# A hybrid decoder trunk on one core: 16x16 blocks of a triangular inverse moved packed, and a short convolution done by tokens from shifted copies in DRAM

## The chip, the cores and the metric

One core of one Trainium2 chip runs the whole program. The metric is the device time of one execution in microseconds; the figure for a kernel is the median of several executions. The profile shows one more execution, with the time of every instruction on the engines: TensorE (PE, its weight loads PEld), VectorE (DVE), ScalarE (ACT), GpSimd (POOL), SyncE (SP). SP does nothing but issue transfers; ACT issues some as well, between its own instructions.

## The reference

Two layers over 256 tokens of width 2048. What matters here is the gated DeltaNet branch:

```
hn   = rms_norm(h, norm_w[l]);  proj = hn @ w_in[l]                 # 8208 columns
qkv  = silu(causal_conv(proj[:, :3072], conv_w))                     # width 4, per channel, over tokens
q, k = l2_norm(q) * 128**-0.5, l2_norm(k);  v = heads(v)             # 8 heads of 128
A    = strict_lower((k * beta) @ k.T * decay)                        # per head, chunks of tokens
u, w = triangular_solve(A + I, [v * beta, k * beta * exp(G)])
...  state recurrence over chunks, o = q_decay @ state + qk @ v_new
y    = concat(gated_head_norm(o, z), hgrn2_branch(...))              # 8 heads each
h    = h + y @ w_out[l]
h    = h + (p[l] @ w_ple_up[l]) * sigmoid(h @ w_ple_gate[l])
```

The other branch (HGRN2) reads the same projection, and a last RMSNorm ends the trunk. All is float32.

## The kernel before

**The matrix products.** Each weight tile is loaded as float32 into a buffer `raw` (three buffers), and split into a high part `whi` (ACT, line 405) and a rest `wlo` (DVE, line 407), three buffers each. A product is three TensorE passes: activation high with weight high, high with rest, rest with high (line 341). The weights are cut into 392 steps in a fixed order (`make_plan`): per layer 128 steps of the input projection, 32 of the output projection, 36 of gate and embedding. A step of 512 columns holds two row tiles of 128 and makes twelve passes of 128x512. `run_step` calls `ahead`, which issues loads up to four steps ahead on SP's queue (line 383) as far as the three buffers allow, and splits two steps ahead, and then makes the step's products.

**The side work.** Everything else is written as generators (`DN`, `HG`, `Inverse`). A generator does a piece of work and yields a number of steps to wait, from the table `DELAY` (overridden per head group by `DELAY_AT`); `tick` at the end of each step counts these down. So their TensorE instructions stand at fixed places between the steps, in the order in which the program issues them. On the other engines a planner orders the instructions at build time by its own estimate of when each is ready, the earlier one of the program first; at run time each engine takes its list in order.

**Values of DeltaNet** (`DN.dv`, four head groups `g` a layer, two heads each). `evict` (line 602) scales the projected values by the row's RMS factor into `vet`; `turned` makes four TensorE transposes into PSUM (`pvc`, line 344), so that tokens lie along the free axis; `conv` then makes the width-4 convolution with two ACT instructions (line 790) and six DVE instructions (line 794), and a sigmoid; line 880 multiplies the two; four more transposes (`pv`) turn the result back, and line 887 scales it by `invn` into `R`. With `R` and the inverse `Tt` the recurrence goes on (`pz`, `pS`, `pw`, `pz`, `po`, then `yt`, `yp` and the split of `y`).

**Inverse** (one per layer, 16 blocks of 128x128 in `Bt`). The 16x16 blocks on the diagonal are inverted by substitution on DVE with one block per partition (`fx`); to get there they go through DRAM: each group's `Bt` is written to `d1` and read back by diagonal blocks. The result goes back the same way: line 659 stores `X` into the diagonal blocks of a DRAM area `d2` that was cleared at the start (line 298, four transfers of 256 KB), and line 661 loads all of `d2`, zeros included, as `Tt` (1 MB), both from ACT's queue and without a yield between. After `T` steps the blocks are merged to 32, 64 and 128 with transposes on DVE (lines 670, 694, 719, 720) and small TensorE products (`pp`, `px`).

**Buffers.** The split activations of every product live in one pool `acts` with 13 buffers of each part: 8 for the normed input, then those of `y`, of the residual, of the embedding. PSUM has three banks for products and five for side work.

## Time and profile before

| | |
|---|---|
| time, median of 3 runs | 1256.82 us (1256.73 to 1257.85) |
| profiled execution, its own time | 1258.06 us |
| its span, first to last instruction | 1256.3 us |
| mean granted clock of TensorE | 0.995 |
| TensorE busy | 1234.1 us (98%), 8385 matmuls |
| VectorE busy | 881.4 us (70%) |
| ScalarE busy | 780.3 us (62%) |
| moved by DMA | 221.59 MB, 176 GB/s over the span |

Busy time is the time in which an engine worked on an instruction; matmuls overlap, so a row of 0.39 us can be followed by the next one 0.23 us later, and the distance of two starts is what a matmul costs. All times in the rows are microseconds from the start of the span unless marked ns.

### The profile page before, as it was taken

The page shows a single profiled execution, that of the slowest core. Times are in us where ns is not written, and L with a number is a line of the kernel's source. Part 1 is how long each engine was busy: PE and PEld are TensorE (multiplying, and loading weights), DVE is VectorE, ACT ScalarE, POOL GpSimd, SP SyncE. Part 2 cuts the span into 40 slices and gives each one's busy share as a digit, 9 for nine tenths or more (in the row PEclk, how much of TensorE's full clock was granted, in tenths as well). Part 3 has the DMA queues.
Part 4 walks back from the last instruction along what each step waited for, and adds up shares of the span by engine and source line. Part 5 has one row for each costly group of instructions (what it writes and reads, how often), then busy time and mean ns, then how long its engine had stood idle before and what let it go on. Part 6 is the DMA issues. An engine that isn't in the chain of part 4 may idle for free.

```text
span 1256.3 us, 21606 instructions
## 1 busy us (share of the span) xinstructions
PE 1234.1 (98%) x8385; PEld 1035.4 (82%) x8385; DVE 881.4 (70%) x1520; ACT 780.3 (62%) x1399; POOL 68.6 (5%) x57
## 2 busy tenths in 40 slices
PE   9999999899999999999999999999999999999996
PEld 7878887698888888888888888887988888888886
DVE  7777796868667755546667877968776596565566
ACT  7567675576666754447556767666776676444465
POOL 0310000000000000000003100000000000000010
PEclk9999999999999999999999999999999999999999
DMA  8565556345455555555565556555455546655563
GB/s 283 191 217 196 177 166 210 121 135 163 141 167 168 167 169 180 190 190 185 185 185 170 176 176 176 171 186 170 124 163 152 170 149 202 195 183 184 184 201 134
DMA packets 76375, 221.59 MB, mean 176 GB/s; under 512 B 15344, under 2 KB 22384, under 8 KB 76272
## 3 DMA queue, kind: packets, MB, share of 16 engines
q1 hardware_dynamic: 59040, 211.52, 53.4%
q10 hardware_dynamic: 17232, 8.69, 2.5%
q8 instruction: 66, 1.08, 0.4%
q14 instruction: 37, 0.30, 0.1%
HBM read 214.67 MB, written 5.51 MB: 175 GB/s over the span
## 4 chain that ended last, share of the span: by engine, by line
PE 85%; DVE 6%; ACT 4%; DMA 3%; issue 2%; ACTq 0%; SPq 0%; DVEq 0%
PE out L341 14%; PE gate L341 13%; PE in1hf L341 7%; PE in1dk L341 7%; PE in0dv L341 6%; PE in1dv L341 6%; PE in0hf L341 5%; PE in1hi L341 5%; PE in0hi L341 4%; PE in0dk L341 4%; DMA raw<-W 3%; DVE wlo L407 2%; PE up L341 2%; ACT whi L405 1%; PE in1dz L341 1%
## 5 line engine op out<-in xcount | busy, mean ns | idle before, releaser
L407 DVE TENSOR_TENSOR wlo<-raw,whi 128x1024 fp32r<-128x1024 f32 (+1 forms) x392 | 482.0, 1232 | 289.2 <-ACT whi L405 287.8
L405 ACT ACTIVATE whi<-raw 128x1024 fp32r<-128x1024 f32 (+1 forms) x392 | 411.7, 1052 | 342.0 <-PE out L341 89.5
L341 PE MATMUL in1hi<-whi,n1hi 128*128 128x512 f32 x128 | 51.5, 403 | 0.0
L341 PE MATMUL in1hf<-whi,n1hi 128*128 128x512 f32 x128 | 51.4, 402 | 0.0
L341 PE MATMUL in1dk<-whi,n1hi 128*128 128x512 f32 x128 | 51.1, 399 | 0.0
L341 PE MATMUL in1hf<-wlo,n1hi 128*128 128x512 f32 x128 | 50.0, 391 | 1.0 <-DVE wlo L407 1.0
L341 PE MATMUL in1hi<-wlo,n1hi 128*128 128x512 f32 x128 | 50.2, 392 | 0.0
L341 PE MATMUL gate<-whi,g0hi 128*128 128x512 f32 x128 | 50.1, 392 | 0.0
L341 PE MATMUL in1hi<-whi,n1lo 128*128 128x512 f32 x128 | 50.0, 390 | 0.0
L341 PE MATMUL in1dk<-whi,n1lo 128*128 128x512 f32 x128 | 50.0, 390 | 0.0
L341 PE MATMUL in1hf<-whi,n1lo 128*128 128x512 f32 x128 | 49.9, 390 | 0.0
L341 PE MATMUL in1dk<-wlo,n1hi 128*128 128x512 f32 x128 | 49.9, 390 | 0.0
L341 PE MATMUL gate<-whi,g0lo 128*128 128x512 f32 x128 | 49.8, 389 | 0.0
L341 PE MATMUL gate<-wlo,g0hi 128*128 128x512 f32 x128 | 49.8, 389 | 0.0
L341 PE MATMUL in1dv<-whi,n1hi 128*128 128x512 f32 (+1 forms) x128 | 48.0, 375 | 0.0
L341 PE MATMUL in1dv<-whi,n1lo 128*128 128x512 f32 (+1 forms) x128 | 46.6, 364 | 0.0
L341 PE MATMUL in1dv<-wlo,n1hi 128*128 128x512 f32 (+1 forms) x128 | 46.5, 363 | 0.0
L341 PE MATMUL gate<-whi,g1hi 128*128 128x512 f32 (+1 forms) x120 | 45.5, 379 | 0.0
L341 PE MATMUL gate<-wlo,g1hi 128*128 128x512 f32 (+1 forms) x120 | 45.4, 379 | 0.0
L341 PE MATMUL gate<-whi,g1lo 128*128 128x512 f32 (+1 forms) x120 | 45.4, 378 | 0.0
L341 PE MATMUL in0hi<-wlo,n0hi 128*128 128x512 f32 x96 | 38.4, 400 | 2.4 <-DVE wlo L407 2.3
L341 PE MATMUL in0hi<-whi,n0hi 128*128 128x512 f32 x96 | 39.2, 409 | 0.0
(1496 smaller groups left out, 3177.9 us busy)
## 6 DMA issues: line engine op xcount, KB each, us to landing
raw<-W SPq DMA_DIRECT2D x384, 512.0 KB, 3.5
raw<-W SPq DMA_DIRECT2D x7, 544.0 KB, 3.7
h<-x SPq DMA_DIRECT2D x4, 512.0 KB, 4.8
xt<-xT SPq DMA_DIRECT2D x3, 512.0 KB, 6.3
out_dram<-h SPq DMA_DIRECT2D x6, 256.0 KB, 2.4
d<-zero ACTq DMA_DIRECT2D x4, 256.0 KB, 7.3
di0d<-di0Bt ACTq DMA_DIRECT2D x4, 256.0 KB, 2.8
di1d<-di1Bt ACTq DMA_DIRECT2D x4, 256.0 KB, 2.3
```

The costliest lines, as they stand in the source:

```text
L341: return tc.keep_in_program_order(nc.tensor.matmul(*a, **k))
L405: S.activation(hi[:, sl], raw[:, sl], AF.Copy)
L407: V.tensor_tensor(lo[:, sl], raw[:, sl], hi[:, sl].bitcast(F32), ALU.subtract)
```

## The change

Four things are changed.

1. The blocks of `Inverse` are moved packed: `X` is stored to `d2` as 128 KB without gaps; after `w` = 2 steps eight transfers on ACT's queue load the diagonal 16x16 blocks from there into `Tt`, 16 partitions each (256 pieces of 64 bytes). The zeros of `Tt` come from four GpSimd memsets at the start of `Inverse.run`. The clearing of the old `d2` is gone. The merge begins 6 steps after the loads (8 after the store), where it began 11 and 13 after.
2. `DN.dv` convolves by tokens, without transposes: `vet` is stored to DRAM (256 KB, ACT's queue) behind three rows of zeros; 2 steps later SP's queue loads the convolution's weights, spread over all partitions (`cvw`, 512 KB, one buffer), and three copies shifted by one, two and three tokens (256 KB each). 3 steps on (5 for group 0 of both layers) DVE makes four multiplications and three additions of 128x512, then the sigmoid, and 2 steps on four instructions of 128x128 that multiply by the sigmoid and `invn` into `R`. `R` is written 8 steps after the group's columns are done (10 for group 0), where it was 6 (7).
3. The loads of the residual input (`xtok`, four of 512 KB on SP's queue) move from steps 22 to 31 to steps 92 to 112 of the loads.
4. `acts` has 12 buffers where it had 13 (the room goes to `cvw`), and some delays change (`h0x4`, `h0o`, `h1c`, `h3q`, `d0z1`, `d1y`, `d1yp`, `d2D`, `i0p32`).

```diff
--- before.py
+++ after.py
@@ -36,23 +36,24 @@
 
 
 DELAY = {
-    "d": {'c': 1, 'D': 4, 'k': 6, 'q': 7, 'ssq': 1, 'v': 5, 'z0': 1, 'S': 1, 'w': 1, 'z1': 1, 'o': 1, 'y': 3, 'yp': 1},
-    "i": {'F': 4, 'F2': 1, 'F3': 1, 'F4': 1, 'T': 12, 't16': 3, 'p16': 2, 't32': 3, 'p32': 2, 't64': 3, 'p64': 2},
+    "d": {'c': 1, 'D': 4, 'k': 6, 'q': 7, 'ssq': 1, 'vl': 2, 'vc': 3, 'v2': 1, 'v': 2, 'z0': 1, 'S': 1, 'w': 1, 'z1': 1, 'o': 1, 'y': 3, 'yp': 1},
+    "i": {'F': 4, 'F2': 1, 'F3': 1, 'F4': 1, 'w': 2, 'T': 6, 't16': 3, 'p16': 2, 't32': 3, 'p32': 2, 't64': 3, 'p64': 2},
     "b": {'o': 1, 'g': 4},
     "h": {'c': 1, 'f': 1, 'x2': 1, 'x4': 1, 'x8': 1, 'a': 2, 'x16': 1, 'x32': 1, 'x64': 1, 'u16': 2, 'u64': 1, 'o': 2, 'y': 2, 'yp': 1, 'q': 0},
 }
 
 DELAY_AT = {
     "b1g": 5,
-    "d0D": 3, "d0c": 2, "d0q": 6, "d0y": 2,
-    "d2D": 3, "d2k": 4, "d2o": 2, "d2q": 9, "d2y": 2,
+    "d0D": 3, "d0c": 2, "d0q": 6, "d0vc": 5, "d0y": 2, "d0z1": 3,
+    "d1y": 4, "d1yp": 3,
+    "d2k": 4, "d2o": 2, "d2q": 9, "d2y": 2,
     "d3D": 5, "d3ssq": 2,
-    "h0c": 2, "h0o": 4, "h0u64": 3, "h0y": 3,
-    "h1c": 3, "h1o": 1, "h1q": 1, "h1x32": 2, "h1yp": 3,
+    "h0c": 2, "h0o": 3, "h0u64": 3, "h0x4": 3, "h0y": 3,
+    "h1c": 4, "h1o": 1, "h1q": 1, "h1x32": 2, "h1yp": 3,
     "h2c": 2, "h2q": 2,
-    "h3u64": 2, "h3x2": 2,
-    "i0T": 11, "i0p16": 1, "i0t16": 5,
-    "i1T": 13, "i1t16": 2,
+    "h3q": 1, "h3u64": 2, "h3x2": 2,
+    "i0p16": 1, "i0p32": 1, "i0t16": 5,
+    "i1t16": 2,
 }
 
 
@@ -164,12 +165,12 @@
-    ap_ = pool("acts", 13)
+    ap_ = pool("acts", 12)
@@ -218,10 +219,10 @@
         7: lambda: x_(3),
         9: lambda: first(cs, cst),
         17: lambda: first(ms, msk),
-        22: lambda: xtok(0),
-        25: lambda: xtok(1),
-        28: lambda: xtok(2),
-        31: lambda: xtok(3),
+        92: lambda: xtok(0),
+        96: lambda: xtok(1),
+        108: lambda: xtok(2),
+        112: lambda: xtok(3),
     }
 
     def first_loads():
@@ -279,7 +280,9 @@
 
     dr = pool("scratch", 1, space=bass.MemoryType.DRAM)
 
-    d2 = dr.tile([16512 * 4 * NG], F32, name="d2")
+    d2 = dr.tile([256 * 128], F32, name="d2")
+
+    dsh = [dr.tile([256 * 259], F32, name=f"dsh{j}") for j in range(2)]
     dfull = lambda d: d.rearrange("(i x) -> i x", i=4 * NG)[:, 0:16384].rearrange("i (p c) -> p i c", c=128)
     ddiag = lambda d: d.rearrange("(q x) -> q x", q=32 * NG)[:, 0:2048].rearrange("q (s f) -> q s f", s=16)[:, :, 0:16]
     SLr = cp.tile([128, 128], F32R, name="SLr")
@@ -287,16 +290,15 @@
     hA = cp.tile([128, 4, 128], F32, name="hA")
 
     def clear_scratch():
+        zero = sp.tile([128, 6], F32, tag="zero", name="zero", bufs=1)
+        G.memset(zero, 0.0)
+        for d in dsh:
+            tc.keep_in_program_order(nc.scalar.dma_start(out=d[0:768].rearrange("(p f) -> p f", p=128), in_=zero))
 
         V.tensor_scalar(SLr, UI, -1.0, 1.0, ALU.mult, ALU.add)
         G.memset(hA[64:128, :, 0:64], 0.0)
         for b in (0, 64):
             G.memset(hA[b + 32:b + 64, :, b:b + 32], 0.0)
-        zero = tp.tile([128, 512], F32, tag="tmp", name="zero")
-        G.memset(zero, 0.0)
-        for j in range(NG):
-            tc.keep_in_program_order(nc.scalar.dma_start(out=dfull(d2)[:, 4 * j:4 * j + 4],
-                                                         in_=zero.rearrange("p (i c) -> p i c", i=4)))
 
     def P(name, i, n=1):
         o = PAR[name][0] + i
@@ -643,6 +645,9 @@
             n, Bt, NT = self.n, self.Bt, self.NT
 
 
+            Tt = self.Tt = v4(mix("Tt", 128 * NT, 1, n + "Tt"))
+            for j in range(0, NT, 4):
+                G.memset(Tt[:, j:j + 4], 0.0)
             fx = tmp(n + "fx").rearrange("q (w a b) -> q w a b", w=2, a=16)
             F, X = fx[:, 0], fx[:, 1]
             nc.scalar.dma_start(out=X, in_=eye)
@@ -656,9 +661,12 @@
                 if c == 1:
                     tc.keep_in_program_order(i)
                 V.tensor_reduce(X[:, :c, c:c + 1], pr_[:, :c, :c], mybir.AxisListType.X, ALU.add)
-            nc.scalar.dma_start(out=ddiag(d2), in_=X)
-            Tt = self.Tt = v4(mix("Tt", 128 * NT, 1, n + "Tt"))
-            nc.scalar.dma_start(out=Tt, in_=dfull(d2))
+
+            nc.scalar.dma_start(out=d2.rearrange("(q a c) -> q a c", q=128, a=16), in_=X)
+            yield self.wait("w")
+            for j in range(8):
+                b = slice(16 * j, 16 * j + 16)
+                nc.scalar.dma_start(out=Tt[b, :, b], in_=d2.rearrange("(i b a c) -> b a i c", i=NT, b=8, a=16)[j])
             yield self.wait("T")
 
 
@@ -874,17 +882,40 @@
 
         def dv(self, ps, c0):
             n, kq, g = self.n, self.kq, self.g
-            et = evict(ps, c0, 256, self.row.rt, n + "v")
-            yield self.wait("c")
-            ac, sg = self.conv(turned(et, 0, n + "pvc"), 2)
-            V.tensor_tensor(ac, ac, sg, ALU.mult)
+
+
+            full = mix("et", 1024, 2, n + "vet")
+            et, x1 = full[:, :512], full[:, 512:]
+            d = dsh[g % 2]
+            for t in range(2):
+                sl = slice(256 * t, 256 * t + 256)
+                S.activation(et[:, sl], ps[t][:, c0:c0 + 256], AF.Copy, scale=self.row.rt[:, t:t + 1])
+            v2 = lambda ap: ap.rearrange("p (t n) -> p t n", t=2)
+            rows = lambda j: d[256 * (3 - j):256 * (259 - j)].rearrange("(t p n) -> p t n", t=2, p=128)
+            nc.scalar.dma_start(out=rows(0), in_=v2(et))
+            wv = mix("cvw", 1024, 1, n + "cvw")
+            yield self.wait("vl")
+            nc.sync.dma_start(out=wv, in_=cvw[self.l * NG + g])
+            xs = [x1, tmp(n + "vs2"), tmp(n + "vs3")]
+            for j, x in enumerate(xs, 1):
+                nc.sync.dma_start(out=v2(x), in_=rows(j))
+            yield self.wait("vc")
+            w = lambda j: bc1(wv[:, 256 * j:256 * j + 256], 2)
+            V.tensor_tensor(v2(et), v2(et), w(3), ALU.mult)
+            for j, x in enumerate(xs, 1):
+                V.tensor_tensor(v2(x), v2(x), w(3 - j), ALU.mult)
+                V.tensor_tensor(et, et, x, ALU.add)
+                if j == 1:
+                    yield self.wait("v2")
+            sigmoid(x1, et)
             yield self.wait("v")
             yield self.after("k")
-            pv = pm.tile([128, 512], F32, tag="m", name=n + "pv")
+
+            R = v4(mix("R", 512, 2, n + "R"))
             for i in range(4):
-                PE.transpose(pv[:, 128 * i:128 * i + 128], ac[:, 128 * i:128 * i + 128], ident)
-            R = v4(mix("R", 512, 2, n + "R"))
-            V.tensor_tensor(R, v4(pv), bc(self.invn, 128), ALU.mult)
+                hh, t = divmod(i, 2)
+                sl = slice(256 * t + 128 * hh, 256 * t + 128 * hh + 128)
+                V.scalar_tensor_tensor(R[:, i], et[:, sl], self.invn[:, i:i + 1], x1[:, sl], ALU.mult, ALU.mult)
             yield lambda: self.inv.ready
             yield self.wait("z0")
             Tt = self.inv.Tt[:, 4 * g:4 * g + 4]
@@ -1389,6 +1420,9 @@
+        "cvw": np.ascontiguousarray(np.broadcast_to(
+            a["dn_conv_w"][:, :, 2048:].reshape(DEPTH, 4, NG, 256).transpose(0, 2, 1, 3).reshape(DEPTH * NG, 1, 1024),
+            (DEPTH * NG, 128, 1024))),
```

## Rows read from the trace of the kernel before

**Rows 1.** The page: busy time of the engines, with their share of the span and their instructions; and the chain that ended last, by engine.

```profile
PE 1234.1 (98%) x8385; PEld 1035.4 (82%) x8385; DVE 881.4 (70%) x1520; ACT 780.3 (62%) x1399; POOL 68.6 (5%) x57
...
PE 85%; DVE 6%; ACT 4%; DMA 3%; issue 2%; ACTq 0%; SPq 0%; DVEq 0%
```

**Rows 2.** The waits of TensorE in the whole span, longest first: who it waited for, us in total, times, the longest.

```profile
PE in0hi L341 <- DVE wlo L407: 2.3, 1, 2.3
PE dn00pg L341 <- DVE dn00kq L802: 1.9, 1, 1.9
PE in0hf L341 <- issue: 1.8, 1, 1.8
PE hg00yp L344 <- DVE hg00yt L580: 1.4, 1, 1.4
...
PE in1hf L341 <- DVE wlo L407: 1.0, 1, 1.0
...
PE di0px L341 <- issue: 0.7, 1, 0.7
```

**Rows 3.** TensorE in order of time around one group of four transposes of the values: start, us, engine, line, operation.

```profile
902.54 0.60 PE L344 MATMUL dn10pvc<-cs,dn10vet 128*128 128x128 f32 x4
902.90 0.48 PE L341 MATMUL in1dv<-whi,n1hi 128*128 128x512 f32 x1
903.21 0.39 PE L341 MATMUL in1dv<-wlo,n1hi 128*128 128x512 f32 x1
903.45 0.40 PE L341 MATMUL in1dv<-whi,n1lo 128*128 128x512 f32 x1
```

**Rows 4.** Three stretches: from:to, length, busy us (x instructions) of PE, PEld, DVE, ACT, POOL, granted clock, DMA share, GB/s. The first two follow the blocks' store and load in layer 0, the last is an even stretch with values of DeltaNet in it.

```profile
200.00:212.00 12.00, 12.00 (x63) 10.32 (x64) 5.62 (x5) 5.97 (x9) 0.00 (x0) 1.00 0.66 229
...
222.00:232.00 10.00, 7.66 (x27) 5.83 (x26) 9.26 (x18) 4.64 (x10) 0.00 (x0) 0.83 0.32 107
...
960.00:990.00 30.00, 30.00 (x144) 25.03 (x143) 17.91 (x27) 19.28 (x35) 1.30 (x1) 1.00 0.55 164
```

**Rows 5.** ACT in order of time in layer 0 from the store of `X` (line 659) to the weight splits that follow; in square brackets the idle time before an instruction and what ended it.

```profile
192.76 0.37 ACTq L659 DMA_DIRECT2D d<-di0fx  x1
...
196.56 0.02 ACT L661 MOVE_SHAPE di0Tt<-d  x1 [1.88 <-DMA d<-di0fx]
196.62 0.81 ACTq L661 DMA_DIRECT2D di0Tt<-d  x1
197.56 1.06 ACT L405 ACTIVATE whi<-raw 128x1024 fp32r<-128x1024 f32 x1 [0.97 <-PE hg00pa L341]
...
207.62 1.06 ACT L405 ACTIVATE whi<-raw 128x1024 fp32r<-128x1024 f32 x1 [5.68 <-DMA raw<-W]
```

**Rows 6.** The same place on TensorE (a step begins at 199.53), and TensorE after its longest wait, which ended at 226.30.

```profile
199.53 0.39 PE L341 MATMUL in0hi<-whi,n0ahi 128*128 128x512 f32 x1
199.93 0.50 PE L341 MATMUL in0hi<-wlo,n0ahi 128*128 128x512 f32 x1
...
227.26 0.63 PE L341 MATMUL in0hi<-wlo,n0hi 128*128 128x512 f32 x1
227.69 0.63 PE L341 MATMUL in0hi<-whi,n0lo 128*128 128x512 f32 x1
```

**Rows 7.** Transfers: target and source, queue, how many, KB each, median us from issue to landing.

```profile
raw<-W SPq DMA_DIRECT2D x384, 512.0 KB, 3.5
...
d<-zero ACTq DMA_DIRECT2D x4, 256.0 KB, 7.3
...
d<-di0fx ACTq DMA_DIRECT2D x1, 128.0 KB, 3.8
...
di0Tt<-d ACTq DMA_DIRECT2D x1, 0.5 KB, 8.1
```

**Rows 8.** The issuing alone of the four transfers that clear `d2`, one behind the other on ACT's queue: ns min/median/max, first and last start.

```profile
L298 ACTq DMA_DIRECT2D d<-zero x4: 393/593/786, 28.2 to 30.2; - x4
```

**Rows 9.** Single DVE operations, ns min/median/max, start, forms: the convolution, a product of 128x512 from SBUF, an instruction of 128x128 with a factor per partition.

```profile
L794 DVE SCALAR_TENSOR_TENSOR dn01vac<-dn01pvc,pr,dn01vac x6: 458/478/482, 312.7 to 315.2; 128x255 f32<-128x255 f32 x2, 128x254 f32<-128x254 f32 x2, 128x253 f32<-128x253 f32 x2
...
L880 DVE TENSOR_TENSOR dn02vac<-dn02vac,dn02vsg x1: 685/685/685, 375.8 to 375.8; 128x512 f32<-128x512 f32 x1
...
L580 DVE SCALAR_TENSOR_TENSOR dn00yt<-dn00o,fo,dn00sz x4: 343/344/352, 327.8 to 328.6; 128x128 f32<-128x128 f32 x4
```

**Rows 10.** One weight step beside the values of group 2 in layer 0, each line from the order of time of its engine: the end of the eviction of these values; the step's load (the second of the two in the row), its split on ACT and on DVE, its second product on TensorE, the first that needs the rest.

```profile
361.75 0.47 ACT L602 ACTIVATE dn02vet<-in0dv,s0rt 128x256 f32<-128x256 f32 x1 [0.52 <-PE in0dv L341]
...
364.82 2.33 SPq L383 DMA_DIRECT2D raw<-W  x2
...
373.63 1.04 ACT L405 ACTIVATE whi<-raw 128x1024 fp32r<-128x1024 f32 x1
...
374.70 1.23 DVE L407 TENSOR_TENSOR wlo<-raw,whi 128x1024 fp32r<-128x1024 f32 x1 [1.65 <-ACT whi L405]
...
379.04 0.40 PE L341 MATMUL in0hf<-wlo,n0hi 128*128 128x512 f32 x1
```

**Rows 11.** TensorE in order of time where its third chunk begins.

```profile
42.93 0.50 PE L341 MATMUL in0dk<-whi,n0ahi 128*128 128x512 f32 x1 [0.73 <-ACT dn00kqet L602]
```

**Rows 12.** The sixth split activation of `y` in layer 0: its transposes on TensorE, and the ACT instruction that reads them.

```profile
L344 PE MATMUL dn02yp<-cs,dn02yt x4: 272/273/273, 407.5 to 407.8; 128*128 128x128 f32 x4
...
L496 ACT ACTIVATE dn02hi<-dn02yp,pr x1: 690/690/690, 415.2 to 415.2; 128x512 fp32r<-128x512 f32 x1
```

More of the change, by code (lines that the diff above doesn't have):

```diff
@@ L166, in trunk @@
 @with_exitstack
-def trunk(ctx: ExitStack, tc: tile.TileContext, head, xT, x, pT, W, par, fw, cst, msk, eye, out):
+def trunk(ctx: ExitStack, tc: tile.TileContext, head, xT, x, pT, W, par, cvw, fw, cst, msk, eye, out):
     nc = tc.nc
```

## The prediction

> **What bounds the kernel now.** I read the page first. TensorE is busy for 98% of the span and makes 85% of the chain that ended last [rows 1]. So only two things can shorten the run: fewer TensorE instructions, or shorter waits of TensorE. Work taken off another engine gains nothing unless TensorE waits for it.
>
> I then read TensorE's waits. They are few, and most stand in one place: the waits for `hg00yt`, for `wlo` under in0hi, for "issue" under in0hf and under di0px [rows 2] all fall between 213 and 243 us, while layer 0's Inverse is in progress. Layer 1 has a single one over 0.3 us there, 1.0 us (in1hf). The remaining one of size, 1.9 us for `dn00kq`, is at the start.
>
> Third, I followed that cluster back on ACT [rows 5]. The store of `X` is issued at 192.76. ACT's next DMA, the load of `Tt`, must wait for it to land: ACT stands idle for 1.88 us and then issues for 0.81 us, so that a weight split starts at 197.56 that could have started at 194.7. Behind it the 1 MB load takes 8.1 us to land [rows 7], and the weight loads share the DMA engines with it: the split at 207.62 comes after 5.68 us of idling for `raw<-W`. DVE and ACT are then a step behind, and TensorE pays up to 30 us later. The DMA share of 0.66 at 229 GB/s [rows 4] puts full DMA at some 229 / 0.66 = 347 GB/s.
>
> **The change: transposes.** Each group of values loses two bursts of four transposes. A burst starts at 902.54 and the next product at 902.90, 0.36 us; that product is followed after 0.31 us by one that would come after 0.23, another 0.08 [rows 3]. With 8 groups and 2 bursts, 16 x 0.44 = 7.1 us leave TensorE. Nothing hides them: it has no idle time beside them.
>
> **The Inverse.** The four waits in layer 0 add up to 2.3 + 1.8 + 1.4 + 0.7 = 6.2 us [rows 2]. A row of idle time counts from the modelled end of a product, 0.39 us after its start, where the next would have started 0.23 us after it [rows 3], so each wait costs 0.16 more: 0.6. After the longest wait products stand 0.43 us apart [rows 6] and the stretch 222 to 232 has a mean granted clock of 0.83 [rows 4]: at half clock (1.2 GHz) that is 0.34 of 10 us, which loses 1.7. Layer 0 pays 8.5 us, layer 1 1.0 + 0.16 = 1.2. The store and the pieces are 128 KB now, the pieces are an eighth of the 1 MB, and two steps (2 x 12 passes x 0.23 = 5.5 us) stand between store and load, where a store of 64-byte pieces landed in 3.8 [rows 7]. The merge moves 3 and 5 steps earlier, so its bursts of small products no longer stand next to those of `hg01pa` or `hg11pa` in the same places; the two waits for "issue" have no other releaser in the profile, and I let them go with the rest, between nothing and all of their 2.8 us. Gain 9.7.
>
> What comes instead is eight issues on ACT's queue in a row, with weight splits queued behind them. One alone takes 0.37 us [rows 5]; the four that clear `d2` grow from 0.39 to 0.79 as they follow each other [rows 8]. So ACT is held for 8 x 0.37 = 3.0 to 8 x 0.79 = 6.3 us, plus between 0 and 1.9 for the store, against 1.88 + 0.81 = 2.7 now. The present hold leaves TensorE just short: at 199.53 the step's first product comes in time, the second, which needs the rest, 0.40 later where 0.23 is normal [rows 6]. So every microsecond more is paid at once, if the planner puts the loads where the old load stood: between 0.3 and 5.5 a layer. Nothing is lost if the two steps move them to a better place, since a split can begin two steps, 5.5 us, before it is needed. I take 2 us a layer, nearer the lower end, because the delay of two steps lies above the landing of 3.8: 4.0 in all.
>
> **Values through DRAM.** On DVE seven instructions of 128x512 at 0.69 and four of 128x128 at 0.34 make 6.2 us; six at 0.48 go, one of 0.69, and line 887, which I price like it: 4.3 [rows 9]. DVE gets 1.9 us more per group and is busy 17.91 of 30 us in a stretch that holds one [rows 4]. Two ACT instructions go and one issue comes. Nothing is added for these.
>
> DMA: 0.25 MB out, 0.75 back and 0.5 of weights per group, 1.5 MB, take 1.5 / 0.347 = 4.3 us of full DMA, on top of 0.55 [rows 4]. On SP's queue weight loads are queued behind them. The slack is read from one weight step: issued at about 366.8, landed by the median 3.5 [rows 7] at 370.3, split from 373.63, the rest done at 375.93, used at 379.04 [rows 10]. That is 3.3 before the split and 3.1 behind it, 6.4 us. The four issues on SP cost 4 x 0.37 = 1.5, the 1.25 MB 3.6: a weight load comes up to 5.1 us later, and the next ones less, since they wait for their buffers. That fits into 6.4 with 1.3 to spare. The wait for the store is the other part: the eviction ends at 362.2, and SP comes to the loads two steps after the group's columns, about when the load at 366.8 goes out; the store may take 3.8 to 7.3 [rows 7], so SP waits between 0 and 2.7. Beyond 1.3 it is paid: 0 to 1.4 a group. I take 0.
>
> **Start.** 1 MB of clearing, 2048 pieces of 512 bytes, goes, with four issues on ACT; the wait for the eviction of `dn00kqet`, 0.73 + 0.16 = 0.9 us [rows 11], should go with it, as ACT and DVE were behind on splits that waited for loads. The wait for `dn00kq` has its causes behind that point on DVE; I leave it, with a bound of 1.9 + 0.16 + 1.7 at half clock = 3.8. Moving the residual's loads moves 2 MB from a stretch without waits to another: nothing, or what the DMA sum above lacks.
>
> **Twelve buffers.** With eight for the normed input, the fifth split of `y` must now wait for the last chunk of the projection, as the sixth does already: transposed at 407.8, read at 415.2 [rows 12]. Each holds a PSUM bank meanwhile, one of five; the values no longer use two. TensorE waits if five are needed at once: between 0 and 7.4 a layer; 0, since the same hold shows no wait today.
>
> **The sum.** Against the execution's 1256.3 span: -7.1 - 9.7 - 0.9 + 4.0 = -13.7. The median of 1256.8 is 0.5 above the span (the profiled execution itself took 1258.06); from the median 1243.1, so I say 1243.
>
> **A rule that speaks against the change.** Four clearing transfers of 256 KB, issued 0.6 apart, landed after 7.3 us in the median [rows 7, 8], so transfers in a row overlap here. The Trainium skill says otherwise of small ones (DMA: Bandwidth & Descriptors, Rules for kernel authors): put many into one large transfer, since under 64 KB one pays mostly overhead. The eight are 16 KB each. No run here shows transfers of that size. The next section prices it from rows.
>
> **Rivals.** (a) The likeliest, 0.42: the sum as it stands, 1239.5 to 1247. (b) 0.17: the eight issues cost TensorE nothing, and the start gains some of its 3.8: 1256.8 - 17.7 = 1239 down to 1235. (c) 0.23: the eight issues stand where the old load stood and hold ACT long, 4 us of wait and 1.7 at half clock per layer: 1256.8 - 17.7 + 11.4 = 1250.5; at the upper bound of 5.5 it is 1253.5. For it: the tight 199.93 [rows 6]. Against: the two steps. (d) Slower, 0.09: SP's queue. If the planner puts the shifted loads before their store has landed, each group's weight loads come later than the 6.4 us of slack; the whole 2.7 wait and as much again by a late eviction give 4.1 too late, with 1.7 at half clock 5.8 us in each of 8 groups: 1243 + 46 = 1289; it passes 1257 from 1.7 us a group on. Against: SP waits for free buffers most of the time, so its lead is small. (e) 0.04: the eight small loads land one behind the other, 8 x 3.8 = 30 us, where 6 steps give 16.3. DVE's first transpose of the merge then waits 14 us with the weight splits behind it; 5.5 of that are covered: 8.5 x 2 + 3.4 at half clock = 20 more, 1263. This is the skill's rule above as a mechanism. (f) 0.05: gains and new waits cancel within the limit, 1254.3 to 1259.3.
>
> **How the numbers follow.** 1243 is (a). For 8 in 10 the range takes (a), the upper part of (b) and (c) up to 1252: 1237 to 1252. By 0.2%, 2.5 us, about what a measurement of this kernel can tell from no change: faster (a), (b), (c) 0.82; same 0.05; slower (d), (e) 0.13.
>
> **What would show it.** Right: 64 matmuls fewer, no idle row of ACT for `raw<-W` near 5 us behind the block loads, granted clock 1.00 from 222 to 232. On ACT the eight issues stand behind a landed store. Wrong: TensorE waiting for `wlo` right behind the eight issues (c), SP idle for the store of `vet` with `whi` waiting for `raw<-W` from 280 to 430 us and in layer 1 (d), DVE idle before line 670 (e), or waits at a PSUM bank around 370 to 415 us.

## The result, and the profile after

The changed kernel takes 1260.8 us (median; 1260.1 to 1264.1) where the kernel before took 1256.8 beside it: ratio 1.0032, 95% interval 1.0019 to 1.0045, slower by some 4 us. I had said 1243. Its profiled execution took 1260.29 us with a span of 1258.6, against 1256.3 before. All rows below are of these profiled executions. (Lines of the code moved: `whi` is now split in line 407, `wlo` in 409, TensorE's products stand in 343.)

The page, engines and chain, answers to [rows 1]:

```profile
PE 1230.1 (98%) x8321; PEld 1029.3 (82%) x8321; DVE 892.4 (71%) x1544; ACT 771.9 (61%) x1381; POOL 71.1 (6%) x65
...
PE 75%; DVE 13%; DMA 5%; ACT 4%; issue 2%; ACTq 0%; SPq 0%; DVEq 0%
```

The 64 products are gone (8385 to 8321), and TensorE is busy for 4 us less. But the chain now runs for 13% through DVE and 5% through DMA, where it was 6% and 3%. Its waits, longest first, answer to [rows 2]:

```profile
PE in0hi L343 <- ACT whi L407: 3.0, 1, 3.0
PE in1hi L343 <- DVE wlo L409: 2.1, 1, 2.1
PE hg12pa L343 <- DVE hg12X L1054: 2.1, 1, 2.1
PE dn00pg L343 <- DVE dn00kq L810: 1.9, 1, 1.9
PE in1hi L343 <- ACT whi L407: 1.8, 1, 1.8
PE in0dz L343 <- ACT whi L265: 1.6, 1, 1.6
PE in0hi L343 <- DVE wlo L409: 1.1, 1, 1.1
```

The old waits for `hg00yt`, for "issue" under in0hf and di0px and for `wlo` 2.3 are gone, as forecast. Four new ones for `whi` and `wlo` stand in their place, two in each layer (3.0 + 1.1 and 2.1 + 1.8). All four come right behind the eight block loads. New too are the wait for `hg12X` (2.1), among layer 1's values, and that of `in0dz` (1.6), at the start. ACT in order of time, layer 0, answers to [rows 5]:

```profile
188.96 0.34 ACTq L665 DMA_DIRECT2D d<-di0fx  x1
...
191.91 5.68 ACTq L669 DMA_DIRECT2D di0Tt<-d  x8
197.69 0.37 ACT L1123 COPY hA<-hg00pa 64x256 f32<-64x256 f32 x1 [6.77 <-DMA di0Tt<-d]
...
199.72 1.99 ACT L407 ACTIVATE whi<-raw 128x1024 fp32r<-128x1024 f32 x2
```

The store lands 2.9 us after its issue, and the loads follow at once. Eight issues hold ACT for 5.68 us, so the next splits start at 199.72. The row has two parts; the first seven and the eighth, each from a window of its own:

```profile
191.91 3.34 ACTq L669 DMA_DIRECT2D di0Tt<-d  x7
...
197.29 0.31 ACTq L669 DMA_DIRECT2D di0Tt<-d  x1
```

Seven issues stand 0.50 apart. The eighth comes 2.0 us after the seventh has ended: it waits for the first of the loads to land (issued at 191.91, landed 5.4 us later at 197.26), whose landing semaphore it uses again. In layer 1 the row holds ACT for 4.74 us. TensorE in order of time:

```profile
197.47 0.39 PE L343 MATMUL in0hf<-whi,n0lo 128*128 128x512 f32 x1
200.81 0.80 PE L343 MATMUL in0hi<-whi,n0ahi 128*128 128x512 f32 x1 [2.96 <-ACT whi L407]
202.75 0.80 PE L343 MATMUL in0hi<-wlo,n0ahi 128*128 128x512 f32 x1 [1.14 <-DVE wlo L409]
203.34 0.63 PE L343 MATMUL in0hi<-whi,n0alo 128*128 128x512 f32 x1
203.77 0.63 PE L343 MATMUL in0hi<-whi,n0ahi 128*128 128x512 f32 x1
```

A step begins at 200.81, after 2.96 us of waiting for its split, and then the products stand 0.43 apart, not 0.23: TensorE is at its lower clock. The two stretches of [rows 4] that follow the loads, with the same columns:

```profile
200.00:212.00 12.00, 10.04 (x35) 7.88 (x36) 7.03 (x9) 6.20 (x8) 0.00 (x0) 0.72 0.44 141
222.00:232.00 10.00, 10.00 (x290) 8.03 (x289) 9.76 (x19) 8.08 (x15) 0.00 (x0) 1.00 0.25 78
```

The granted clock from 222 to 232 is 1.00 now, as I had said, and the slow stretch has moved to 200 to 212 (0.72). A second engine stood still as well; DVE in order of time:

```profile
198.48 1.43 DVE L678 STREAM_TRANSPOSE di0T<-di0Tt 32x512 f32<-32x512 f32 x2 [5.13 <-DMA di0Tt<-d]
...
201.47 3.59 DVE L409 TENSOR_TENSOR wlo<-raw,whi 128x1024 fp32r<-128x1024 f32 x3
```

DVE had the merge's first transposes next and waited 5.13 us for the pieces to land, with three weight splits behind them.

To see where time goes or comes, the table has the start of eight weight steps and of the last product, in us from the start of the span in the kernel before (from TensorE's order of time), and for the other kernels the difference. Each row is one execution, which can lie off its kernel's median (the most here: sp_late_t, 1242.9 against 1246.1). Steps 188 and 810 lie ahead of the block loads, 215 and 839 behind them, 293 and 922 behind the merge, 467 and 1082 begin the output projections.

```
kernel          188.0  215.3  293.2  466.6  809.7  838.6  921.7 1081.8 1246.5
changed          -2.6   +2.8   -2.8   -2.7   -4.4   +5.7   +1.6   +1.5   +1.6
inv_only         -0.4   +3.0   -2.9   -2.8   -2.9   +4.1   +2.3   +2.3   +2.3
inv_sp           -2.1   -2.0   -7.7   -7.5   -7.6   -5.1   -7.3   -7.3   -7.3
val_only         -1.7   +6.1   +4.1   +5.8   +4.0   +5.0   +8.7   +9.3  +10.3
after_sp         -2.8   -4.4  -10.1   -9.6  -11.4   -8.6  -12.7  -12.6  -12.5
t_late           -1.0   +2.9   -2.9   -2.7   -4.5   +3.4   -0.6   -0.9   -0.8
sp_tlate         -2.5   -4.0   -9.7  -10.9  -12.7   -9.8  -13.9  -12.5  -12.3
act_half         -1.2   -2.4   -8.1   -8.2  -10.0   -7.0  -11.0  -11.0  -10.9
act_apart        -2.1   -3.0   -2.6   +1.6   -0.2   +0.9   -1.4   -1.4   -1.2
no_shift         -2.3   -3.9   -9.7  -11.3  -13.1  -10.4  -13.7  -15.1  -15.0
no_store_wait    -1.1   -2.7   -8.6   -7.3   -9.1   -6.4  -10.6   -7.4   -6.9
sp_late_t        -2.4   -4.0   -9.8  -11.8  -13.2  -10.5  -14.4  -16.4  -15.5
```

The changed kernel loses 5.4 us between 188 and 215 and 10.1 between 810 and 839. Not all of that is loss: the new delays move small products of TensorE across these marks. Those of `hg00pa`, in the kernel before and in the changed one:

```profile
186.81 1.31 PE L341 MATMUL hg00pa<-hg00X 128*32 128x16 f32 x64
```

```profile
190.98 1.20 PE L343 MATMUL hg00pa<-hg00X 128*32 128x16 f32 x64
```

They stand ahead of step 188 in the kernel before and in inv_only and inv_sp, behind it in the others; `hg10pa` does the same at 810. So the first table's marks compare only kernels with the same delays. A second table is cut at places where all its kernels have made the same small products (the values' transposes apart). It has what each stretch of the kernel before gains or loses, from the same executions. Layer 0's Inverse lies in 172 to 286 and its values in 286 to 467, layer 1's in 790 to 901 and 901 to 1082.

```
kernel          0-66  66-172  172-286  286-467  467-790  790-901  901-1082  1082-end
changed         +1.0    -2.0     -1.7      0.0     +0.1     +5.1      -1.0      +0.1
inv_only        -0.4    -0.1     -2.5     +0.1      0.0     +5.0      +0.1       0.0
inv_sp          -0.4    -1.7     -5.6     +0.1      0.0     +0.2      +0.1       0.0
after_sp        +0.7    -2.0     -8.7     +0.4     +0.1     -2.3      -0.8      +0.1
t_late          +0.8    -0.3     -3.3      0.0     +0.1     +2.9      -1.1       0.0
sp_tlate        +1.1    -2.0     -8.6     -1.3     +0.1     -2.1      +0.5       0.0
act_half        +0.7    -0.4     -8.3     -0.2     +0.1     -2.0      -0.9       0.0
act_apart       +1.4    -2.0     -1.6     +3.8     +0.1     -2.2      -0.8       0.0
no_shift        +1.2    -2.0     -8.7     -1.8     +0.1     -2.3      -1.6       0.0
no_store_wait   +0.8    -0.3     -8.6     +0.9     +0.1     -2.1      +2.1      +0.3
```

Between 66 and 172 some 1.7 of the gain is not the change's. TensorE waits 1.9 us there for `dn00kq` in every kernel, and the clock behind it falls in the profiled execution of some (9 of the 20) and not of the others. Before, and changed:

```profile
68.00:76.00 8.00, 6.38 (x22) 5.13 (x23) 5.73 (x15) 4.25 (x14) 0.64 (x1) 0.79 0.82 271
```

```profile
68.00:76.00 8.00, 6.08 (x34) 5.04 (x32) 5.82 (x15) 5.89 (x16) 0.03 (x1) 1.00 0.64 199
```

inv_only, t_late, act_half and no_store_wait fell as the kernel before did.

### The profile page after: what moved, and what is told of

Read it like the earlier page. It is cut to its first block, busy times and chain, and to the rows that moved or that the text cites. A ratio compares the mean times of both kernels' runs of the same rounds, so it can differ in the third digit from the quotient of the medians.

```text
span 1258.6 us, 21543 instructions
## 1 busy us (share of the span) xinstructions
PE 1230.1 (98%) x8321; PEld 1029.3 (82%) x8321; DVE 892.4 (71%) x1544; ACT 771.9 (61%) x1381; POOL 71.1 (6%) x65
## 4 chain that ended last, share of the span: by engine, by line
PE 75%; DVE 13%; DMA 5%; ACT 4%; issue 2%; ACTq 0%; SPq 0%; DVEq 0%
PE out L343 14%; PE gate L343 13%; PE in1dk L343 7%; PE in1hf L343 5%; PE in0dk L343 5%; DVE wlo L409 5%; PE in1dv L343 5%; PE in1hi L343 4%; PE in0hf L343 3%; PE in0hi L343 3%; PE in0dv L343 3%; PE up L343 2%; DMA raw<-W 1%; ACT whi L407 1%; PE in1dz L343 1%
## 5 line engine op out<-in xcount | busy, mean ns | idle before, releaser
L343 PE MATMUL in0hf<-whi,n0hi 128*128 128x512 f32 x96 | 38.4, 400 | 0.0
```

Source lines behind the costliest of these rows:

```text
L343: return tc.keep_in_program_order(nc.tensor.matmul(*a, **k))
```

## The experiments

The kernel before was timed beside every group of runs and moved between 1257.3 and 1258.7, so the ratio compares better than the median.

| kernel | median us | ratio to before, 95% interval |
|---|---|---|
| inv_only | 1258.9 | 1.0007, 0.9996 to 1.0018 |
| val_only | 1270.4 | 1.0101, 1.0084 to 1.0119 |
| inv_sp | 1251.9 | 0.9959, 0.9943 to 0.9975 |
| after_sp | 1247.5 | 0.9920, 0.9903 to 0.9936 |
| act_spread | 1261.1 | 1.0018, 1.0008 to 1.0028 |
| t_late | 1257.5 | 0.9994, 0.9981 to 1.0008 |
| sp_tlate | 1246.8 | 0.9914, 0.9893 to 0.9934 |
| act_dep | 1258.1 | 1.0005, 0.9990 to 1.0021 |
| act_half | 1248.7 | 0.9923, 0.9905 to 0.9941 |
| act_apart | 1259.0 | 1.0007, 0.9993 to 1.0022 |
| no_shift | 1243.8 | 0.9879, 0.9862 to 0.9896 |
| no_store_wait | 1249.8 | 0.9932, 0.9916 to 0.9948 |
| sp_order | 1254.2 | 0.9957, 0.9941 to 0.9974 |
| vl_late | 1247.4 | 0.9903, 0.9887 to 0.9918 |
| sp_late | 1245.8 | 0.9905, 0.9886 to 0.9925 |
| sp_late_t | 1246.1 | 0.9899, 0.9880 to 0.9919 |
| sp_vhold | 1245.5 | 0.9900, 0.9882 to 0.9918 |
| sp_late_vhold | 1251.1 | 0.9947, 0.9932 to 0.9961 |

### Which part costs, and is it the queue

The theory (H): the issues on ACT. The rival (V): the values through DRAM. Each part alone, and each kernel with the loads on the other queue:

```diff
-                nc.scalar.dma_start(out=Tt[b, :, b], in_=d2.rearrange("(i b a c) -> b a i c", i=NT, b=8, a=16)[j])
+                nc.sync.dma_start(out=Tt[b, :, b], in_=d2.rearrange("(i b a c) -> b a i c", i=NT, b=8, a=16)[j])
```

**inv_only** (the kernel before with the diff's Inverse, its delays and without the clearing of `d2`): 

> The kernel before with the packed Inverse alone: store of X packed, memset of Tt, eight block loads issued by ACT, no clearing of d2; the values stay on the old path. Theory H (the eight issues hold ACT for 5.7 us a layer and TensorE pays about 7 us for it in each layer, in place of the 8.5 and 1.2 us that it waited before): -9.7 - 0.9 + 14.2 = +3.6, so about 1260, with ACT's next instruction waiting some 6 us behind the eight issues and TensorE waiting for whi or wlo right there. Rival V (the Inverse is worth what I forecast, and the values through DRAM eat it): -9.7 - 0.9 + 4.0 = -6.6, about 1250.

**inv_sp** (the same with the edit above): 

> As the kernel before with the packed Inverse alone, but the eight block loads are issued on SP's queue. Theory H: nothing holds ACT, so -9.7 - 0.9 plus at most 2 for weight loads queued behind the eight issues on SP: 1246 to 1249. If small pieces landing late or the merge itself were what costs the time (rival S), it stays within 2 us of the same kernel with the issues on ACT.

**after_sp** (the changed kernel with the edit above): 

> The changed kernel with one edit: the eight block loads are issued on SP's queue and not on ACT's. Theory H: the stalls of about 7 us behind the issues in each layer go, 1260.8 - 14.2 + at most 3 = 1247 to 1250. Rival S (small pieces or the merge cost the time) and rival V (the values do): 1258 to 1261.

**val_only** (the changed kernel with the Inverse, the clearing and the delays `F` to `T` of before): 

> The changed kernel with the old Inverse (1 MB through DRAM, d2 cleared, its old delays): the values by tokens alone, with the twelve buffers and the later residual loads. Theory H: the 64 transposes give back 7.1 us, and the late weight loads behind SP's waits for the store take most of it, so 1250 to 1257. Rival V: 1263 or more, since the values then cost 6 us or more net of the transposes.

One word, scalar or sync, is worth 0.0112 of the time in the changed kernel: 14 us by the ratios, 13.3 by the medians, as H says. In the table the loss at the block loads goes from +5.4 to -1.6 and from +10.1 to +2.8, 7.0 and 7.3 us a layer, and nothing else moves by a microsecond. SP and DVE in order of time in after_sp:

```profile
191.50 3.77 SPq L669 DMA_DIRECT2D di0Tt<-d  x8
```

```profile
195.08 0.70 DVE L678 STREAM_TRANSPOSE di0T<-di0Tt 32x512 f32<-32x512 f32 x1 [0.29 <-DMA di0Tt<-d]
...
197.07 1.23 DVE L409 TENSOR_TENSOR wlo<-raw,whi 128x1024 fp32r<-128x1024 f32 x1 [1.29 <-DMA di0Tt<-d]
```

SP issues the same eight in 3.77 us where ACT took 5.68, so DVE's wait shrinks too, and two suspects left together: the next runs part them. With the Inverse alone the queue is worth 6 us by the ratios: there the issues held ACT for 3.9 us, not 5.7, since the first load had landed when the eighth's turn came.

The 13 us of val_only don't price the values. Most of its loss stands between 188 and 215 (7.8 us), at the old 1 MB load, where DVE comes too early to the merge. DVE in order of time:

```profile
202.62 1.42 DVE L677 STREAM_TRANSPOSE di0T<-di0Tt 32x512 f32<-32x512 f32 x2 [6.35 <-DMA di0Tt<-d]
204.07 2.36 DVE L414 TENSOR_TENSOR wlo<-raw,whi 128x1024 fp32r<-128x1024 f32 x2
```

In the kernel before DVE came to this later. The old Inverse under the new order has a wait of its own, so this run can't tell the parts apart. after_sp against inv_sp can, by stretches: where the values stand, after_sp is 0.3 us behind inv_sp in layer 0 and 0.9 ahead in layer 1. The rest of what it gains on inv_sp stands elsewhere.

### ACT's hold or DVE's early wait

Rival E: DVE's transposes, ahead of the splits in its order. Each is held back until the last product that stands ahead of it in the program has run (`not_before` adds that wait):

```diff
                 i = V.transpose(Tn[b:b + 32], Tt[b:b + 32, :, b:b + 32])
+                not_before(i, PE.last)
```

**t_late** (the changed kernel with this): 

> In the trace of the changed kernel two engines stand still together: ACT for the row of eight issues (5.7 us), and DVE, which has the merge's first transposes in its order right behind the loads and waits 5.1 us for the last piece to land, with the weight splits behind it. This kernel is the changed one, the eight issues on ACT as they are, but each of the four transposes also waits for the last product that stands ahead of it in the program, six steps after the loads, so DVE does the splits first. Theory H (ACT's row of issues is what is paid): 1257 to 1261. Theory E (DVE's early wait for the landing is what is paid, my rival (e) at a smaller price): 1246 to 1251. Both in series: between, near 1254.

**sp_tlate** (and the loads on SP): 

> The block loads on SP (1247.5 without more) and the transposes held back in the same way. Theory H: within 1.5 us of 1247.5, since DVE waits only 0.3 and 1.3 us there. Theory E: 1 to 3 us faster, 1244.5 to 1246.5.

ACT and DVE in order of time in t_late:

```profile
193.33 5.27 ACTq L675 DMA_DIRECT2D di0Tt<-d  x8
198.70 0.37 ACT L1130 COPY hA<-hg00pa 64x256 f32<-64x256 f32 x1 [6.38 <-DMA di0Tt<-d]
```

```profile
200.85 0.42 DVE L1055 TENSOR_TENSOR hg00X<-hg00X,hg00k 128x256 f32<-128x256 f32 x1 [6.10 <-ACT hg00X L1053]
```

DVE no longer waits for the landing. It waits as long for ACT. Between t_late and sp_tlate, which differ in the queue alone, lie 10 us by the ratios and 10.7 by the medians, 5.4 and 5.0 a layer at the block loads. ACT's hold (with the wait for a landing that is in it) is the main price, and DVE's early wait added the rest (4.8 by the ratios, 3.3 by the medians). With the loads on SP holding the transposes back gives nothing measurable.

### Every issue, or only a row of them

```diff
                 nc.scalar.dma_start(out=Tt[b, :, b], in_=d2.rearrange("(i b a c) -> b a i c", i=NT, b=8, a=16)[j])
+                if j in (1, 3, 5):
+                    yield 1
```

**act_spread** (with `T` 3 for 6): 

> The changed kernel, the eight block loads still on ACT's queue, but two at a time with one step between the pairs; the merge starts as late as before (three steps after the last pair in place of six). If what costs TensorE is the row of eight on ACT (5.7 us at once, while a weight split has some 5.5 us of lead), pairs of 1.5 us each fit into the lead and nearly all of the 13.3 us come back that moving the loads to SP gave: 1247 to 1250. If every microsecond on ACT is paid wherever it stands, it stays at 1258 to 1261.

**act_dep** (t_late, and each pair also behind `not_before(i, PE.last)`): 

> As the kernel before this one, and the eight issues stand on ACT in pairs one step apart, each held by a wait for a product (in the run where only the program had them apart they were put in a row again: 5.6 us, 0.77 apart). Theory H: pairs of 1.5 us fit into the lead of a split, 1247 to 1250, 10 us less than with the row. Theory E: no more than 2 us from the kernel with the row and the late transposes.

Both missed because the edit didn't take: ACT in order of time in act_spread has one row again, and act_dep one of 5.47 us.

```profile
192.08 5.64 ACTq L669 DMA_DIRECT2D di0Tt<-d  x8
```

A delay says how late a piece of work stands in the program; the planner may still issue it as soon as its data is there. So two more:

**act_half** (t_late with `(nc.scalar if j % 2 == 0 else nc.sync)`): 

> The changed kernel with the transposes held back, and the eight block loads issued in turn by ACT and SP, four on each. With all eight on ACT that kernel took 1257.5, with all on SP 1246.8, 5.4 us a layer between them. If the row on ACT is paid only beyond the lead of a split, four issues (2 to 3 us) cost almost nothing: 1246 to 1249. If each issue is paid, half of it: 1251 to 1253.

**act_apart** (act_dep with two steps between pairs): 

> The changed kernel with the transposes held back and all eight issues on ACT, in pairs two steps apart (each pair waits for a product; one step apart they still stood in a row of 5.5 us). If the trace shows them apart: only beyond the lead, 1246 to 1250; each issue paid, 1256 to 1259. If ACT is blocked by those waits themselves, slower than 1260.

ACT in act_half:

```profile
193.07 1.91 ACTq L675 DMA_DIRECT2D di0Tt<-d  x4
195.03 0.63 ACT L1053 ACTIVATE hg00X<-hg00X 128x512 f32<-128x512 f32 x1 [2.92 <-DVE hA L1129]
```

Four issues in 1.91 us, none waiting for a landing, cost nothing that can be seen: the loss at the block loads is that of sp_tlate within 0.3 us in each layer, and the ratio within the intervals. In act_apart the pairs stand apart:

```profile
192.10 0.84 ACTq L675 DMA_DIRECT2D di0Tt<-d  x2
...
193.02 0.93 ACTq L675 DMA_DIRECT2D di0Tt<-d  x2
...
204.88 0.91 ACTq L675 DMA_DIRECT2D di0Tt<-d  x2
```

and between 188 and 215 all eight on ACT cost 0.6 us (-0.9 in the table, beside -1.5 in sp_tlate); in layer 1 they cost nothing over the whole stretch (790 to 901: -2.2, in sp_tlate -2.1). So only what goes beyond a split's lead is paid. By its total, 1259.0, the run sides with "each issue paid"; the loss stands elsewhere: the merge of layer 0 now comes later (the first product of `di0px` at 231.7, in sp_tlate at 222.0) and meets the small products of `hg01`, and TensorE's waits have a row of

```profile
PE hg01pa L343 <- issue: 3.3, 1, 3.3
```

and the gain behind the merge (293 and 467 in the table) is gone. That the later merge is the cause was not tried by itself. My forecast "only beyond the lead" was right for the place of the loads and wrong for the total.

### What the way through DRAM costs

**no_shift** (after_sp without store and shifted loads): 

> The changed kernel with the block loads on SP, without the store of the values and the three shifted loads of each group: 1 MB a group less over DMA, no wait for the store on SP, four issues less. DVE does as many operations of the same size, on the weights in place of the shifted copies, so the convolution is not computed. If the way through DRAM is hidden (as I forecast), it comes out within 1 us of the same kernel with it, 1247.5. If the waits for the store or the DMA traffic cost TensorE what the transposes gave (1.8 to 5 us), 1243 to 1246.

```diff
-                nc.sync.dma_start(out=v2(x), in_=rows(j))
+                nc.sync.dma_start(out=v2(x), in_=xin[j][:, :, 0:256])
```

**no_store_wait** (after_sp with this): 

> The changed kernel with the block loads on SP (1247.5), and the three shifted loads of each group read rows of the input x in place of the stored values, in pieces of the same 1 KB; the store still goes out. Traffic and issues are as before, but SP never waits for the store; the convolution is not that of the values. If SP's wait (5.4 us at most) is what the way through DRAM costs, it comes near the kernel without store and loads: 1243 to 1245. If it is the traffic, it stays: 1246.5 to 1248.5.

In no_store_wait the shifted loads read the input `x` (`xin`) in place of the stored values; the store stays, and nothing waits for it.

Leaving store and loads out gives 0.0041, 5 us by the ratios (3.6 by the medians, 2.5 in the traces). SP's waits and ACT's waits for loaded weights in after_sp:

```profile
SPq L901 <- DMA dsh<-dn02vet: 5.4, 1, 5.4
SPq L901 <- DMA dsh<-dn12vet: 4.6, 1, 4.6
```

```profile
ACT whi L407 <- DMA raw<-W: 41.4, 28, 6.8
```

and in no_store_wait the latter, and TensorE's longest waits:

```profile
ACT whi L409 <- DMA raw<-W: 23.1, 19, 2.4
```

```profile
PE hg12pa L345 <- DVE hg12X L1056: 3.7, 1, 3.7
PE hg02pa L345 <- DVE hg02X L1056: 2.1, 1, 2.1
```

Without SP's wait the weights come in time again, 23.1 us of waiting for 41.4, and the kernel is no faster (0.9932 against 0.9920). TensorE's waits for late splits at 365 us in after_sp (0.4 and 0.9) shrink to 0.3, about 1 us, and those for `hg02X` and `hg12X` grow from 0.8 and 2.2 to 2.1 and 3.7. So the wait and the late weights are the smaller part of what TensorE pays. The run does not price them cleanly: without the dependence the planner may also order DVE otherwise. DVE ahead of hg12pa in after_sp, where TensorE waits 2.2 us:

```profile
916.62 1.54 DVE L904 TENSOR_TENSOR dn11vet<-dn11vet,dn11cvw 128x512 f32<-128x512 f32 x1 [1.62 <-DMA dn11cvw<-cvw]
918.09 1.21 DVE L409 TENSOR_TENSOR wlo<-raw,whi 128x1024 fp32r<-128x1024 f32 x1
...
920.30 0.42 DVE L1054 TENSOR_TENSOR hg12X<-hg12X,hg12q 128x256 f32<-128x256 f32 x1
```

DVE waits for the convolution's weights of group 1 (one buffer, so their load waits until group 0 is done with it), with `hg12X` behind. Four kernels moved parts of this:

```diff
-            nc.sync.dma_start(out=wv, in_=cvw[self.l * NG + g])
+            tc.keep_in_program_order(nc.sync.dma_start(out=wv, in_=cvw[self.l * NG + g]))
```

```diff
-    'vl': 2, 'vc': 3, 'v2': 1, 'v': 2
+    'vl': 4, 'vc': 3, 'v2': 1, 'v': 1
```

**sp_order** (after_sp, the first edit): 

> The changed kernel with the block loads on SP, and with the load of the convolution's weights kept in the order of the program on SP, since the trace shows that of the first group (512 KB) issued 2.2 us into the span, ahead of the first weights. The first product of step 1 stands at 6.2 us there, at 2.1 in the kernel with the Inverse alone. If this load causes it, step 1 comes 2 us earlier; what is left of that at the end lies between 0.5 and 2, so 1245.5 to 1247. If the first loads are late for another reason, 1247.5.

**vl_late** (both edits): 

> As the kernel with the block loads on SP and the weights in order, and the loads of the shifted copies come two steps later, one step of which the end of the group's values gives back. SP should not wait for the store any more. If those waits (4.1 to 5.7 us in four groups) cost time, 1 to 4 us are gained, 1242 to 1245.5; if they stand in SP's lead, it is within 1 us of that kernel, or slower by what the later values cost.

**sp_late** (after_sp, the second): 

> The block loads on SP and the loads of the shifted copies two steps later, with nothing pinned in SP's order. If SP's waits for the store (5.4 and 4.6 us the longest) are what the way through DRAM costs, it keeps most of the 2.6 to 4 us that leaving store and loads out gave: 1243.5 to 1245.5. If its price is the traffic or the planner's placing of DVE's work, 1246.5 to 1248.5.

**sp_late_t** (sp_tlate, the second): 

> Block loads on SP, transposes held back, loads of the shifted copies two steps later in the program: the three edits that each gave something or nothing. If they add up, 1244 to 1246; if the late transposes only helped where the issues stood on ACT, as 1246.8 against 1247.5 says, it lies at the 1245.8 of the late loads alone.

sp_order's step 1 does start 1.4 us earlier than after_sp's (first products at 9.5 and 10.9, and at 9.0 in inv_only; the 6.2 and 2.1 of my expectation are no such starts), and 0.9 of it is left at 66 us; behind that its profiled execution falls to the lower clock and after_sp's does not. The kernel came out slower by 0.0037 with the pinned order, and has new waits for `dn00v` and `dn10v` (1.6 and 1.3 us). Its trace is of the fastest execution, 1249.1 where the median is 1254.2, so it does not show all of that. vl_late, with the pin, is faster than sp_order by 0.0054; against after_sp it can't be told apart. In sp_late SP waits for the store as long as before (5.4 us): again the delay did not move the issue. But DVE comes to the values later there, the rows for hg02X and hg12X are gone, and with the late transposes as well, in sp_late_t, the last product comes earlier (table: -15.5 against -12.3 in sp_tlate, but of executions 3.2 and 0.8 us below their medians). sp_late_t has the lowest ratio of the kernels that do all the work, 0.9899, some 13 us below the kernel before and 17 below the changed one; its interval holds sp_tlate, vl_late, sp_late and sp_vhold too.

Last, DVE's first product of the values held back alone:

```diff
-            V.tensor_tensor(v2(et), v2(et), w(3), ALU.mult)
+            i = V.tensor_tensor(v2(et), v2(et), w(3), ALU.mult)
+            not_before(i, PE.last)
```

**sp_vhold** (sp_tlate with this): 

> Block loads on SP and the merge's transposes held back (1246.8), and DVE's first product of the values' convolution also waits for the last product of TensorE that stands ahead of it in the program, so DVE cannot come to it before the convolution's weights have landed. If DVE's early wait for those weights is what costs TensorE its waits for hg02X and hg12X (0.5 and 2.0 us), these rows go and it gains 2 to 3 us: 1244 to 1245. If DVE's added work itself is the cause, the rows stay and it is within 1 us of 1246.8.

**sp_late_vhold** (sp_late_t with this): 

> The same with the loads of the shifted copies two steps later (1246.1 without the new wait, where the two rows for hg02X and hg12X are gone already). Within 1 us of 1246.1 if those rows were all that the wait costs; faster than 1245 if DVE's other waits for the shifted copies (0.8 and 2.1 us) cost too.

In sp_vhold the row for hg02X is gone and that for hg12X is 1.2 us, for 2.0; the time is within the intervals of sp_tlate (0.9900 against 0.9914). DVE's early wait has its part in these rows, and its price can't be told from nothing. sp_late_vhold is 6 us slower than sp_late_t, and TensorE's waits name it:

```profile
PE dn00pz L343 <- DVE dn00R L926: 2.4, 1, 2.4
PE dn10pz L343 <- DVE dn10R L926: 2.1, 1, 2.1
```

Now group 0's values are too late for the recurrence. Its place has a few microseconds on either side, and DVE's order decides which is paid.

## Why the prediction was wrong, by its own steps

**Transposes, -7.1: right as work, and not to be seen in the time.** Each of the 16 bursts of the kernel before takes 0.35 or 0.36 us to the next product and delays the one behind it as in [rows 3], 7.1 us in all, and they are gone. But in the two stretches that held them the changed kernel gains 0.0 and 1.0, after_sp -0.4 and 0.8. What ate the rest stands under the values.

**The eight issues, +4.0: the step that failed.** I took 2 us a layer "because the delay of two steps lies above the landing of 3.8". The delay did nothing of the sort: the planner issued the row the moment the store had landed, where the old load had stood and where [rows 6] had shown no slack. The row cost 7.0 and 7.4 (changed against after_sp in 172 to 286 and in 790 to 901), 14.4 in all, 10.4 above the term: some 5 a layer for ACT's hold, the lower clock in it, the other 2 for DVE. In size this is rival (c) at its upper bound of 5.5 + 1.7 a layer, but part of that is luck. The bound took each issue to grow to 0.79; they stood 0.50 apart, and the hold of 5.68 in layer 0 has 2.0 us in it in which the eighth waited for the first to land, a term I did not have. The share of DVE, which waits for the landing with splits behind it, I had under rival (e) alone. The eight small loads did not land one behind the other: 16 KB each, median 4.9 us from issue to landing, with 0.50 between the first seven issues. DVE still stood in front of line 678 for 5.1 us.

**The Inverse, -9.7: right.** after_sp shows what is left when no row of issues is in the way: it gains 8.7 us in layer 0's stretch (8.5 forecast) and 2.3 in layer 1's (1.2 forecast), 11.0 in all, and TensorE's waits between 172 and 286 are gone. The packed Inverse alone does not give this. inv_sp gains 5.6 and loses 0.2: it keeps the wait of 0.7 for "issue" at di0px and shorter ones for `wlo` (0.8) and `hg00yt` (0.3), and in layer 1 waits 1.6 for `wlo` where it waited 1.0. Of the rest of the change, the moved delays act in these stretches; that they make the difference was not tried.

**Start, -0.9: the wait went, the time did not.** TensorE no longer waits for the eviction of [rows 11]. But the changed kernel is 1.7 us late from 17 to 40 us and still 1.0 late at 66, so the term came out at +1.0. The convolution's weights of the first group, which wait for nothing, went out ahead of the first weights (512 KB at 2.2 us); with that load pinned, sp_order is 0.1 early at 66. I had not seen that a load without a cause to wait can be moved to the start. What the changed kernel gains behind that, 2.0, is mostly the clock of this execution of the kernel before.

**Values through DRAM, 0: the second step that failed.** The stretches that hold the values lose 6.1 of the transposes' 7.1 us in the changed kernel and 6.7 in after_sp. SP did wait for the store, 5.7 us at most where I had said 2.7, and weights came late as rival (d) has it: ACT's splits wait 14.1 us for `raw<-W` between 280 and 430, where they waited 2.6. The slack of [rows 10] held most of it: in after_sp the late splits cost TensorE 1.3 us, at 365. The larger price stood where I had written "nothing is added": DVE, whose `hg02X` and `hg12X` TensorE awaits for 0.8 and 2.2. Without the store and the shifted loads 3.0 us come back in these stretches (5 by the ratios). How the rest divides between DVE's early waits, its longer work and the clock stays open.

**The sum with what was measured:** +1.0 and -2.0 up to 172, -11.0, +14.4, -1.0 where the values stand, +0.2 elsewhere = +1.6 at the last product; the span grew by 2.3. No run takes the twelve buffers or the residual's loads apart. Between 370 and 415 us TensorE waits for a PSUM bank once, 0.3 us at `in0dv` for the eviction of `hg03fqet`. The residual's loads now go out between 304 and 373 us, among the values of layer 0, where they went between 65 and 95; what they add to the late weights there is not known.

**The chances:** I gave (c) 0.23 against 0.42 for the sum, with the row that spoke for it in hand, and the range ended at 1252 while (c)'s upper bound alone gave 1253.5. The 6 us lost on the values came on top.

## What to carry to other kernels

Count every issue of a transfer as work of the engine that issues it, and if a row of issues exceeds the lead of what is queued behind it, give it to an engine whose queue has slack: one word was worth 14 us here. See whether an issue of the row waits for an earlier one to land. A delay in the program is a hope, not a bound, where a planner orders the work; a load with nothing to wait for goes to the front, an operation with its data on the way goes ahead of work that was ready. When two engines stand still together, one experiment that frees both proves neither; hold each back by itself. When stretches of two kernels are compared, cut them where both have done the same work, and look at the clock of both executions.

## What the runs showed of the hardware

Issues of 16 KB in pieces of 64 bytes follow each other after 0.50 us on ACT's queue (0.37 behind the first), and after 0.49 on SP's (after_sp). One issue of the packed store took 0.34. In the changed kernel's layer 0 the eighth on ACT starts at 197.29, 0.03 after the first has landed, and both use the same landing semaphore; t_late, act_spread and act_dep show the same (0.02 after the landing). In inv_only the first lands at 197.43, the eighth's turn comes at 198.56, and there is no gap. A row of seven was not tried. In layer 1 one issue of the row takes 1.3 us, in after_sp on SP too (1.2); the cause is open.

The Trainium skill (DMA: Bandwidth & Descriptors, Issuing engines are not separate DMA queues) says that issuing from another engine only saves the sequencer's time to start the transfer, and that this is usually small beside the transfer. For one transfer the runs agree: 0.50 us of issuing, 4.9 to landing (median). A row adds up: eight held ACT for 5.7 us, 3.7 of issuing and 2.0 of waiting for a landing, and moving them to SP was worth 14 us.

In the changed kernel a stall of 2.96 us and one of 1.14 behind it were followed by products 0.43 us apart where 0.23 is normal, TensorE's lower clock of 1.2 GHz (granted clock 0.72 from 200 to 212 us); in after_sp, without the stall, they were not (1.00 from 200 to 212). The wait of 1.9 us for `dn00kq` is in the traces of all 20 kernels; the clock behind it fell in 9 of them (0.79 from 68 to 76 us in the kernel before) and stayed at 1.00 in 11.
